# Layer norm closings with a full-array mean, statistics as columns and a diagonal matrix

## The chip, the cores and the metric

One core of one Trainium2 chip runs the whole program. The metric is the device time of one execution in microseconds, smaller is better. The engines are PE (TensorE, products), DVE (VectorE), ACT (ScalarE), POOL (GpSimd) and SP (SyncE, which issues most transfers). Each engine works off its own list of instructions in order.

## What is computed

The program is the backbone of a diffusion transformer: two layers, 256 latent and 256 context tokens of width 1024. Each layer is a half-step feed-forward block, four token mixers side by side, and a second feed-forward block. Every sub-layer ends in a residual with a layer norm behind it, which is what the change is about:

```python
def _norm_f32(x):
    xf = x.astype(jnp.float32)
    mu = jnp.mean(xf, axis=-1, keepdims=True)
    var = jnp.mean(jnp.square(xf - mu), axis=-1, keepdims=True)
    return (xf - mu) * lax.rsqrt(var + LN_EPS)
...
def residual(h, y, mods, s, g, b, r):
    return layer_norm(ALPHA * h + r * mods[..., s, 2, :] * y, g, b)
...
        h_ctx = residual(h_ctx, swiglu_ffn(modulate(h_ctx, mod_c, 0), ffn_w_in[l, 0], ffn_w_out[l, 0]),
                         mod_c, 0, ln_g[l, 0], ln_b[l, 0], FFN_RES)
```

In the last layer the context stream ends inside the mixer, so that mixer 1 and the last feed-forward block work on the 256 latent tokens alone. The convolution mixer has a layer norm of width 512 in its middle.

## The kernel before

**Layout.** Activations are held transposed: `ah` is eight tiles of 128 features (on the partitions) by 512 columns, two *sets* of 256 columns for the two streams. A product in full precision is made as three products of split operands (`xh`, `xl` for the high and low part of the activations, `hi`, `lo` for those of the weights), each a row `mm<-xh,hi` and so on. Products of fp32 operands, as those of the statistics, run as two passes each.

**Order.** The code is written in an order of its own, and a scheduler places the instructions on each engine's list when the program is built; what stands there is what the engine then does, one after another. Inside the mixers a budget (`work`, counted by `mm` and by `counted`) also decides which piece of a branch is written next, so that an operation of another size can move others.

**A norm.** Class `Norm` (L259) serves all layer norms. `arrive(m, cs)` takes in tile m of a residual when it is complete: it squares it (`sq`) and adds the square and the tile itself to running sums `self.q` and `self.s` on DVE (rows `sq<-sq,sq` and `lns<-lns,ah`). `finish(s)` is the *closing* of set s. It sums over the features, which lie on the partitions, by products with a constant matrix `ones[n]` that holds 1/n: four products `st` put mean square and mean as rows onto partitions 0 and 32 of one PSUM tile. ACT copies the mean out (`lnm`, 64x128), DVE squares it and subtracts (`lnv`), ACT takes the root (Sqrt with `eps`), DVE the reciprocal (L311). Row vectors are spread over all partitions by products with a selector, a column of the identity that is broadcast: `bcm` spreads the mean and `bcr` the reciprocal deviation, two products each. `center` subtracts `bcm` from a tile, `scale` multiplies it by `bcr`; ACT then modulates it (`xf`), rounds it (`xh`), and DVE forms the rest (`xl`).

**Where closings stand.** There are 13. Eight belong to four *two-set boundaries* (behind feed-forward block 0 and mixer 0 of layer 0, behind its second block, and behind the first block of layer 1): the set that is complete first is closed first (the *first closing*), and the late output tiles of the other set run as products beside it; then comes the *second closing* in `Boundary.prep` (L431), and the next sub-layer's products have begun on the first set by then. Three stand in the convolution mixers (L772, width 512). Two are *one-set closings*: mixer 1's layer norm (L1159) and the very last, whose scaled tiles are the output. In `ffn` the norm is made at L527.

Of the kernel before, what the change touches and what calls it, by code (L numbers as in the profile page):

```python
# [10 lines left out]
F32 = mybir.dt.float32  # L11
# [6 lines left out]
T = 256  # L18
# [42 lines left out]
def trunk_kernel(ctx: ExitStack, tc: tile.TileContext, I: dict, out: bass.AP):  # L61
# [18 lines left out]
    class Lower:  # L80


        def __init__(self, t):
            self.t = t
# [67 lines left out]
    def sel(r):  # L152

        return ident[0:64, r:r + 1].to_broadcast([64, 128])

# [103 lines left out]
    class Norm:  # L259
# [3 lines left out]
        def __init__(self, n, tiles, pre=False):  # L263
            self.n, self.tiles, self.pre, self.bc = n, tiles, pre, {}

        def arrive(self, m, cs):
# [18 lines left out]
            if m == 0:  # L285
                self.q = sq
            else:
                if m == 1:
                    self.s = blk("lns")
                tt(out=self.q[:, cs], in0=self.q[:, cs], in1=sq[:, cs], op=ALU.add)  # L290
                tt(out=self.s[:, cs], in0=(self.tiles[0] if m == 1 else self.s)[:, cs], in1=d[:, cs], op=ALU.add)

        def finish(self, s):

            H = slice(0, 64)
            p = aux("st")
            for i, x in enumerate((self.q, self.s)):
                for q in range(2):
                    mm(p[32 * q:32 * q + 32, i * 128:i * 128 + 128], ones[self.n][:, 0:32],
                                     x[:, s * T + q * 128:s * T + q * 128 + 128], start=True, stop=True)  # L300
            e2, mu = p[H, 0:128], p[H, 128:256]
            m = sp.tile([64, 128], F32, tag="lnm", name=nm("lnm"), bufs=2)
            v = sp.tile([64, 128], F32, tag="lnv", name=nm("lnv"), bufs=2)
            b, c = aux("bcm"), aux("bcr")
            act(m, mu, AF.Copy)
            tt(out=v, in0=m, in1=m, op=ALU.mult)
            for q in range(2):
                mm(b[:, q * 128:q * 128 + 128], sel(32 * q), m, start=True, stop=True)
            tt(out=v, in0=e2, in1=v, op=ALU.subtract)
            act(v, v, AF.Sqrt, bias=eps[H])  # L310
            V.reciprocal(v, v)  # L311
            for q in range(2):
                mm(c[:, q * 128:q * 128 + 128], sel(32 * q), v, start=True, stop=True)
            self.bc[s] = b[:, 0:T], c[:, 0:T]
# [209 lines left out]
    def ffn(l, w, bd, first, cs, order, np_, nm_=1):  # L524

        s = 2 * w
        nrm = Norm(1024, ah, True)  # L527
# [46 lines left out]
    def mixer(l, bd, cs, sets, order):  # L574
# [584 lines left out]
        nrm = Norm(1024, ah, True)  # L1159
# [161 lines left out]
```

## Time and profile before

| | |
|---|---|
| time, median of 3 runs | 2272.79 us (2269.57 to 2275.2) |
| profiled execution | 2276.33 us, its span 2274.1 us |
| mean granted clock of PE | 0.993 |
| PE busy | 2222.4 us, 98% |
| DVE busy | 1634.6 us, 72% |
| ACT busy | 946.8 us, 42% |
| bytes moved | 323.23 MB, mean 142 GB/s |

The busy times are sums over one profiled execution; the span runs from its first to its last instruction. An engine that is busy 98% of the span sets the time; of the others it matters only where that engine waits for them.

### The profile page before, as it was taken

Reading aid. Unit: us, or ns where it says so; the run is one execution under the profiler, and the core shown is the slowest. Engines: PE = TensorE matmul, PEld = TensorE weight load, DVE = VectorE, ACT = ScalarE, POOL = GpSimd, SP = SyncE. Lnnn points to the kernel's source line nnn. Section 1 sums busy time; section 2 is a strip of 40 time slices with the busy share of each in tenths; the row PEclk is TensorE's granted clock in tenths of the full one; section 3 lists DMA queues with packets and bytes.
Section 4 is the critical chain, followed back from the end, with each engine's and each line's share of the span. In section 5 each row is a group of like instructions: output and inputs, shape, how many; then the busy total and the mean of one; then the engine's idle time right before and its main releaser. Section 6 shows DMA issues by size and latency. Waiting matters only on the chain.

```text
span 2274.1 us, 31541 instructions
## 1 busy us (share of the span) xinstructions
PE 2222.4 (98%) x12216; PEld 1908.5 (84%) x12216; DVE 1634.6 (72%) x2881; ACT 946.8 (42%) x1476; POOL 19.7 (1%) x82
## 2 busy tenths in 40 slices
PE   7999999999999999999999999999999999998997
PEld 4788788888888888888888888888889998998997
DVE  6997865768995754695747488766558989776656
ACT  5322132642345753362222244222326645755443
POOL 2000000000000000000000000000000000000000
PEclk9999999999999999999999999999999999999999
DMA  8665652223222132235535426554534643354653
GB/s 307 214 223 184 204 166 93 98 85 119 85 97 89 57 102 93 84 125 163 168 120 167 139 75 189 181 164 149 160 102 131 190 138 113 121 177 135 197 182 99
DMA packets 94454, 323.23 MB, mean 142 GB/s; under 512 B 10592, under 2 KB 12640, under 8 KB 94304
## 3 DMA queue, kind: packets, MB, share of 16 engines
q1 hardware_dynamic: 94304, 321.22, 43.7%
q8 instruction: 96, 1.57, 0.3%
q14 instruction: 54, 0.44, 0.1%
HBM read 320.12 MB, written 1.05 MB: 141 GB/s over the span
## 4 chain that ended last, share of the span: by engine, by line
PE 89%; DVE 6%; ACT 2%; issue 1%; DMA 1%; SPq 0%; ACTq 0%; DVEq 0%
PE mm L122 84%; DVE lo L113 2%; PE num L122 1%; ACT hi L125 1%; DVE junk L366 1%; DVE junk L216 1%; DVE cacc L113 1%; DVE ah L113 1%; PE gt L122 0%; PE ax L122 0%; PE qk L122 0%; DMA raw<-in_ffn_out 0%; PE bcm L122 0%; DVE sq L113 0%; PE bcr L122 0%
## 5 line engine op out<-in xcount | busy, mean ns | idle before, releaser
L125 ACT ACTIVATE hi<-raw 128x1024 fp32r<-128x1024 f32 (+1 forms) x462 | 474.9, 1031 | 1059.6 <-PE mm L122 709.5
L122 PE MATMUL mm<-xh,hi 128*128 128x512 f32 (+1 forms) x2448 | 847.2, 349 | 7.2 <-ACT hi L125 3.0
L122 PE MATMUL mm<-xh,lo 128*128 128x512 f32 (+1 forms) x2448 | 848.8, 348 | 4.5 <-DVE lo L113 4.5
L122 PE MATMUL mm<-xl,hi 128*128 128x512 f32 (+1 forms) x2448 | 848.4, 347 | 0.0
L113 DVE TENSOR_TENSOR lo<-raw,hi 128x1024 fp32r<-128x1024 f32 (+1 forms) x462 | 546.3, 1186 | 258.3 <-ACT hi L125 255.0
L122 PEld LDWEIGHTS mm<-xh,hi 128*128 128x128 f32 x2448 | 461.9, 190 | 68.3 <-ACT hi L125 5.2
L122 PEld LDWEIGHTS mm<-xh,lo 128*128 128x128 f32 x2448 | 464.4, 190 | 64.4 <-DVE lo L113 6.9
L122 PEld LDWEIGHTS mm<-xl,hi 128*128 128x128 f32 x2448 | 464.9, 190 | 57.0 <-issue 0.7
L122 PE MATMUL mm<-gh,hi 128*128 128x512 f32 (+1 forms) x1600 | 406.6, 344 | 4.2 <-ACT gh L125 2.8
L216 DVE CUSTOM_DVE_ANT_0 junk<-ada,cbc 128x1024 bf16<-128x1024 f32 x256 | 313.0, 1223 | 98.3 <-DMA ada<-in_wada 94.8
L122 PEld LDWEIGHTS mm<-gh,hi 128*128 128x128 f32 x1600 | 277.1, 189 | 46.8 <-ACT gh L125 3.7
L122 PE MATMUL mm<-gh,lo 128*128 128x512 f32 (+1 forms) x800 | 276.0, 345 | 0.0
L122 PEld LDWEIGHTS mm<-gh,lo 128*128 128x128 f32 x800 | 151.1, 189 | 20.2 <-issue 0.7
L113 DVE SCALAR_TENSOR_TENSOR ah<-mm,gate,ah 128x256 f32<-128x256 f32 x192 | 86.1, 480 | 104.5 <-PE mm L122 104.1
L113 DVE SCALAR_TENSOR_TENSOR cacc<-pd,cw,cacc 128x512 f32<-128x512 f32 (+1 forms) x240 | 133.2, 614 | 0.2
L122 PE MATMUL mm<-yh,hi 128*128 128x512 f32 (+1 forms) x512 | 129.3, 339 | 0.0
L113 DVE TENSOR_TENSOR sg<-sg,mm 128x512 f32<-128x512 f32 (+1 forms) x87 | 53.8, 618 | 78.1 <-PE mm L122 77.3
L122 PEld LDWEIGHTS mm<-yh,hi 128*128 128x128 f32 x512 | 88.1, 189 | 11.3
L122 PE MATMUL mm<-yh,lo 128*128 128x512 f32 (+1 forms) x256 | 86.5, 338 | 0.0
L125 ACT ACTIVATE gh<-sg 128x512 fp32r<-128x512 f32 (+1 forms) x88 | 50.5, 574 | 53.2 <-DVE sg L113 52.9
L122 PE MATMUL mm<-mh,hi 128*128 128x256 f32 (+1 forms) x320 | 67.0, 307 | 0.9 <-DVE mh L113 0.6
L125 ACT ACTIVATE xf<-ah,bp,gp 128x256 f32<-128x256 f32 x88 | 48.6, 592 | 24.1 <-DVE ah L113 19.1
(241 smaller groups left out, 1759.8 us busy)
## 6 DMA issues: line engine op xcount, KB each, us to landing
raw<-in_ffn_in SPq DMA_DIRECT2D x176, 512.0 KB, 3.5
ada<-in_wada SPq DMA_DIRECT2D x136, 512.0 KB, 4.0
raw<-in_ffn_out SPq DMA_DIRECT2D x64, 512.0 KB, 3.6
raw<-in_w_G SPq DMA_DIRECT2D x64, 512.0 KB, 3.3
raw<-in_w_br SPq DMA_DIRECT2D x32, 512.0 KB, 3.3
raw<-in_ffn_out SPq DMA_DIRECT2D x32, 384.0 KB, 3.5
raw<-in_w_o SPq DMA_DIRECT2D x24, 512.0 KB, 3.3
shw<-in_wshift SPq DMA_DIRECT2D x16, 256.0 KB, 5.8
```

The lines of the kernel that those rows point to most:

```text
L113: return f(*a, **k)
L122: nc.tensor.matmul(o, w, x, **kw)
L125: S.activation(o, i, f, **kw)
L216: V.tensor_tensor_reduce(out=cur["junk"], in0=w, in1=cur["c"][:, v], scale=1.0, scalar=0.0, op0=ALU.mult, op1=ALU.add, accum_out=m[:, v, t ...
L366: V.tensor_tensor_reduce(out=cur["junk"], in0=w, in1=cur["c"][:, v], scale=1.0, scalar=0.0, op0=ALU.mult, op1=ALU.add, accum_out=m[:, v, k ...
```

## The change

**The mean** is spread by one full-array product of `ones[n]` with the running sum, 256 columns, straight into `bcm`; it reads no result of ACT. **The statistics** are made as columns, tokens on the partitions: products in which the sums are the weights (128 columns) and two columns of `ones[n]` move, four for each pair of sums, into eight columns of `bcr`'s bank beyond the part that is used for the spread. ACT squares the mean (128x4), DVE subtracts, ACT takes the root, DVE the reciprocal, all on 128x4. **The deviation** is spread by way of a diagonal matrix: two DVE operations multiply the identity by the columns of the reciprocal and by n (`dg`, 128x128 each), and one product of `ones[n]` with `dg` gives `bcr`. In norms of one set (`alone`) the last tile and its square aren't added to the sums by DVE: PE adds them up in PSUM, by a second `bcm` product and four more products for the statistics. `sel` goes, a tile `st` less is taken from PSUM in each closing, a block for `dg` more from SBUF.

```diff
...
@@ -260,8 +256,8 @@

 

-        def __init__(self, n, tiles, pre=False):
-            self.n, self.tiles, self.pre, self.bc = n, tiles, pre, {}
+        def __init__(self, n, tiles, pre=False, alone=False):
+            self.n, self.tiles, self.pre, self.alone, self.bc = n, tiles, pre, alone, {}

         def arrive(self, m, cs):
             d = self.tiles[m]
@@ -283,34 +279,41 @@
             if m == len(self.tiles) - 2 and self.pre:
                 act(sp.tile([128, 1], F32, tag="dmy", name=nm("dmy"), bufs=1), sq[:, cs.start:cs.start + 1], AF.Sqrt)
             if m == 0:
-                self.q = sq
+                self.q, self.s = [sq], []
+            elif m == len(self.tiles) - 1 and self.alone:
+
+                self.q.append(sq)
+                self.s.append(d)
             else:
                 if m == 1:
-                    self.s = blk("lns")
-                tt(out=self.q[:, cs], in0=self.q[:, cs], in1=sq[:, cs], op=ALU.add)
-                tt(out=self.s[:, cs], in0=(self.tiles[0] if m == 1 else self.s)[:, cs], in1=d[:, cs], op=ALU.add)
+                    self.s.append(blk("lns"))
+                a, b = self.q[0], self.s[0]
+                tt(out=a[:, cs], in0=a[:, cs], in1=sq[:, cs], op=ALU.add)
+                tt(out=b[:, cs], in0=(self.tiles[0] if m == 1 else b)[:, cs], in1=d[:, cs], op=ALU.add)

         def finish(self, s):

-            H = slice(0, 64)
-            p = aux("st")
-            for i, x in enumerate((self.q, self.s)):
-                for q in range(2):
-                    mm(p[32 * q:32 * q + 32, i * 128:i * 128 + 128], ones[self.n][:, 0:32],
-                                     x[:, s * T + q * 128:s * T + q * 128 + 128], start=True, stop=True)
-            e2, mu = p[H, 0:128], p[H, 128:256]
-            m = sp.tile([64, 128], F32, tag="lnm", name=nm("lnm"), bufs=2)
-            v = sp.tile([64, 128], F32, tag="lnv", name=nm("lnv"), bufs=2)
+            n, cs = self.n, vcols(s)
             b, c = aux("bcm"), aux("bcr")
-            act(m, mu, AF.Copy)
-            tt(out=v, in0=m, in1=m, op=ALU.mult)
-            for q in range(2):
-                mm(b[:, q * 128:q * 128 + 128], sel(32 * q), m, start=True, stop=True)
+            for i, x in enumerate(self.s):
+                mm(b[:, 0:T], ones[n], x[:, cs], start=i == 0, stop=i == len(self.s) - 1)
+
+            ops = [(j, x, t) for i in range(len(self.q)) for j, x in ((0, self.q[i]), (1, self.s[i])) for t in range(2)]
+            for i, (j, x, t) in enumerate(ops):
+                o, k = T + 4 * j + 2 * t, s * T + t * 128
+                mm(c[:, o:o + 2], x[:, k:k + 128], ones[n][:, 0:2], start=i == 0, stop=i == len(ops) - 1)
+            e2, mu = c[:, T:T + 4], c[:, T + 4:T + 8]
+            v = sp.tile([128, 4], F32, tag="lnv", name=nm("lnv"), bufs=2)
+            act(v, mu, AF.Square)
             tt(out=v, in0=e2, in1=v, op=ALU.subtract)
-            act(v, v, AF.Sqrt, bias=eps[H])
+            act(v, v, AF.Sqrt, bias=eps)
             V.reciprocal(v, v)
-            for q in range(2):
-                mm(c[:, q * 128:q * 128 + 128], sel(32 * q), v, start=True, stop=True)
+
+            dg = blk("dg")
+            for t in range(2):
+                ts(out=dg[:, t * 128:t * 128 + 128], in0=ident, scalar1=v[:, 2 * t:2 * t + 1], scalar2=float(n),
+                   op0=ALU.mult, op1=ALU.mult)
+            mm(c[:, 0:T], ones[n], dg[:, 0:T], start=True, stop=True)
             self.bc[s] = b[:, 0:T], c[:, 0:T]

         def center(self, m, s, o):
@@ -524,7 +527,7 @@
     def ffn(l, w, bd, first, cs, order, np_, nm_=1):

         s = 2 * w
-        nrm = Norm(1024, ah, True)
+        nrm = Norm(1024, ah, True, len(order) == 1)
         xh, xl = first[:2] if bd is None else (bd.xh, bd.xl)
         rest = None
         for pi, (j0, j1) in enumerate(PARTS):
@@ -1156,7 +1159,7 @@
             gh.append(a)
             gl.append(b)
         finish_gate(l, 1)
-        nrm = Norm(1024, ah, True)
+        nrm = Norm(1024, ah, True, nset == 1)

         def evac(m, p, c, vs):
             resid(m, p, l, 1, vs)
```

Counted over the program, PE has 26 `bcm`, 26 `bcr` and 52 `st` products fewer, and 15 `bcm` and 13 `bcr` products over 256 columns and 60 two-column products more. DVE has 13 reciprocals and 26 multiplications or subtractions on 64x128 and four additions on 128x256 fewer, and 13 reciprocals, 13 subtractions on 128x4 and 26 `dg` operations more. Three loads of an activation table fewer are on ACT.

PE at the second closing of the first boundary, before (`mm` are products of the next sub-layer on the first set, `st`, `bcm` and `bcr` the closing's; 22 rows of `mm` are left out):

```order
L122 MATMUL mm_2972<-xh_2921,lo_2969 128x256
L122 MATMUL st_3132<-sq_2659,ones_81 32x128 x2
L122 MATMUL st_3132<-lns_2696,ones_81 32x128 x2
L122 MATMUL bcm_3139<-lnm_3137,ident 128x128 x2
L122 MATMUL mm_2951<-xh_2922,hi_2947 128x256
...
L122 MATMUL bcr_3140<-lnv_3138,ident 128x128 x2
L122 MATMUL mm_2972<-xh_2923,lo_2969 128x256
```

and the same place after the change:

```order
L122 MATMUL mm_2972<-xh_2921,lo_2969 128x256
L122 MATMUL bcm_3130<-lns_2696,ones_81 128x256
L122 MATMUL bcr_3131<-ones_81,sq_2659 128x2 x2
L122 MATMUL bcr_3131<-ones_81,lns_2696 128x2 x2
L122 MATMUL bcr_3131<-dg_3142,ones_81 128x256
L122 MATMUL mm_2951<-xh_2922,hi_2947 128x256
L122 MATMUL mm_2958<-xh_2922,hi_2954 128x256
L122 MATMUL mm_2965<-xh_2922,hi_2961 128x256
L122 MATMUL mm_2972<-xh_2922,hi_2968 128x256
L122 MATMUL mm_2951<-xl_2930,hi_2947 128x256
```

Before, 23 rows of `mm` lay between `bcm` and `bcr`; now `bcr` stands directly behind the statistics, and the first row that needs an `xl` is the fifth behind it. The other three boundaries read the same.

DVE at the same closing, before (`ah<-ah,bcr` scales the first set, `ah<-ah,bcm` centers the second):

```order
L113 TENSOR_TENSOR ah_108<-ah_108,bcr_2981 128x256
L113 TENSOR_TENSOR lnv_3138<-lnm_3137 64x128
L113 TENSOR_TENSOR xl_2930<-xf_3150,xh_2922 128x256
L113 TENSOR_TENSOR lnv_3138<-st_3132,lnv_3138 64x128
L113 TENSOR_TENSOR ah_109<-ah_109,bcr_2981 128x256
```

and after the change:

```order
L113 TENSOR_TENSOR lnv_3137<-bcr_3131,lnv_3137 128x4
L113 TENSOR_TENSOR ah_108<-ah_108,bcr_2974 128x256
L310 RECIPROCAL lnv_3137<-lnv_3137 128x4
L113 TENSOR_TENSOR ah_109<-ah_109,bcr_2974 128x256
L113 TENSOR_SCALAR dg_3142<-ident,lnv_3137 128x128 x2
L113 TENSOR_TENSOR ah_102<-ah_102,bcm_3130 128x256
L113 TENSOR_TENSOR ah_103<-ah_103,bcm_3130 128x256
L113 TENSOR_TENSOR ah_104<-ah_104,bcm_3130 128x256
L113 TENSOR_TENSOR xl_2930<-xf_3146,xh_2922 128x256
```

The difference `xl_2930` has moved from the middle of the chain to a place behind `dg` and three centers.

PE in the last mLSTM head of mixer 1, before (`C` is the state's product, `qk` the scores', `M` and `w` spread gates, `num` the numerator; `mm` the dense products of the output branches):

```order
L122 MATMUL mm_16460<-xh_13390,lo_16406 128x256
L122 MATMUL C_16274<-vaug_14908,kw_16263 128x129
L122 MATMUL qk_16281<-q_16153,k_16098 128x256
L122 MATMUL C_16274<-vaug_14908,kw_16263 128x129 x3
L122 MATMUL qk_16281<-q_16153,k_16098 128x256
L122 MATMUL M_16287<-Mw_15571,identr 128x256
L122 MATMUL w_16297<-Mw_15572,identr 128x256
L122 MATMUL M_16300<-Mw_15571,identr 128x256
L122 MATMUL w_16310<-Mw_15572,identr 128x256
L122 MATMUL num_16346<-vaug_14908,E_16291 128x129
```

and after the change, where rows of `mm` lie in the places left out:

```order
L122 MATMUL C_16193<-vaug_14884,kw_16172 128x129 x4
L122 MATMUL qk_16206<-q_16126,k_16079 128x256 x2
...
L122 MATMUL M_16212<-Mw_15547,identr 128x256
L122 MATMUL bcr_16178<-dg_16189,ones_79 128x256
...
L122 MATMUL w_16263<-Mw_15548,identr 128x256
...
L122 MATMUL M_16305<-Mw_15547,identr 128x256
...
L122 MATMUL w_16354<-Mw_15548,identr 128x256
...
L122 MATMUL num_16357<-vaug_14884,E_16216 128x129
```

The rows left out hold 17, 15, 23, 7 and 6 `mm` products; before, none stood between `C` and `num`. The transposes `kT` ahead of them have moved some 70 rows forward.

## Rows read from the trace of the kernel before

**Rows 1.** The page's first part: engine, busy us (share), instructions.

```profile
PE 2222.4 (98%) x12216; PEld 1908.5 (84%) x12216; DVE 1634.6 (72%) x2881; ACT 946.8 (42%) x1476; POOL 19.7 (1%) x82
```

**Rows 2.** PE's waits: line, awaited line, total us, times, longest us.

```profile
PE st L122 <- DVE sq L113: 6.6, 6, 1.8
PE bcr L122 <- DVE lnv L311: 3.4, 2, 1.7
```

**Rows 3.** Like operations elsewhere: tiles `dn`, `bp`; timeline of `hs`, `hT`, `qk`.

```profile
L113 DVE TENSOR_TENSOR dn<-num,dn x24: 127/153/159, 739.0 to 1965.9; 128x2 f32<-128x2 f32 x24
L1051 DVE RECIPROCAL dn<-dn x24: 131/158/168, 739.4 to 1966.5; 128x2 f32<-128x2 f32 x24
...
L125 ACT ACTIVATE bp<-shift,cols x8: 240/262/263, 14.9 to 50.8; 128x2 f32<-128x2 f32 x8
...
805.91 0.86 DVE L113 TENSOR_SCALAR hs<-hs,hmv,hrs 128x128 f32<-128x128 f32 x3
...
861.67 1.25 PE L1090 MATMUL hT<-ident,hs 128*128 128x128 f32 x10
...
1932.39 1.03 PE L122 MATMUL qk<-q,k 128*128 128x256 f32 x4
```

**Rows 4.** Tile `lnv`: shortest, median, longest ns, first and last start.

```profile
L113 DVE TENSOR_TENSOR lnv<-lnm x13: 275/282/285, 398.9 to 2262.7; 64x128 f32<-64x128 f32 x13
...
L311 DVE RECIPROCAL lnv<-lnv x13: 935/939/946, 400.2 to 2264.1; 64x128 f32<-64x128 f32 x13
```

**Rows 5.** Timeline, second closing, first boundary: start, us, instructions, [idle before <-releaser].

```profile
413.73 0.36 PE L122 MATMUL mm<-xh,hi 128*128 128x256 f32 x1 [0.56 <-DVE ah L113]
...
415.23 0.42 DVE L113 TENSOR_TENSOR sq<-sq,sq 128x256 f32<-128x256 f32 x1
...
415.56 1.41 DVE L113 TENSOR_TENSOR ah<-ah,bcr 128x256 f32<-128x256 f32 x4
...
415.79 0.41 PE L122 MATMUL st<-sq,ones 128*32 128x128 f32 x4 [0.76 <-DVE sq L113]
...
416.01 0.41 PE L122 MATMUL st<-lns,ones 128*32 128x128 f32 x4
...
416.82 0.71 PE L122 MATMUL bcm<-lnm,ident 64*128 64x128 f32 x4 [0.40 <-ACT lnm L125]
...
419.00 0.64 PE L122 MATMUL mm<-xh,hi 128*128 128x256 f32 x4
...
420.41 0.71 PE L122 MATMUL bcr<-lnv,ident 64*128 64x128 f32 x4
...
421.05 0.39 PE L122 MATMUL mm<-xh,lo 128*128 128x256 f32 x1
```

**Rows 6.** Timeline, mixer 1's one-set closing.

```profile
2058.88 0.41 PE L122 MATMUL st<-sq,ones 128*32 128x128 f32 x4 [1.80 <-DVE sq L113]
...
2059.55 0.27 ACT L125 ACTIVATE lnm<-st 64x128 f32<-64x128 f32 x1 [1.49 <-PE st L122]
...
2062.45 1.22 PE L122 MATMUL bcr<-lnv,ident 64*128 64x128 f32 x4 [1.70 <-DVE lnv L311]
...
2065.61 1.22 PE L122 MATMUL mm<-xh,hi 128*128 128x256 f32 x4 [1.95 <-ACT xh L125]
```

**Rows 7.** Window behind it: us; PE, PEld, DVE, ACT, POOL busy; PEclk, DMA, GB/s.

```profile
2066.00:2070.00 4.00, 4.00 (x20) 4.00 (x20) 3.54 (x12) 4.00 (x10) 0.00 (x0) 0.50 0.00 0
```

**Rows 8.** Timeline, the last closing.

```profile
2265.11 1.22 PE L122 MATMUL bcr<-lnv,ident 64*128 64x128 f32 x4 [1.70 <-DVE lnv L311]
...
2266.91 1.07 DVE L113 TENSOR_TENSOR ah<-ah,bcr 128x256 f32<-128x256 f32 x3
```

**Rows 9.** Mixer 1's last mLSTM head: timeline of PE, then two windows.

```profile
1960.41 0.38 PE L122 MATMUL w<-Mw,identr 128*128 128x256 f32 x1 [0.78 <-DVE qw L113]
...
1959.00:1963.00 4.00, 2.68 (x11) 2.15 (x11) 3.94 (x10) 4.00 (x12) 0.00 (x0) 0.79 0.38 131
1963.00:1966.00 3.00, 3.00 (x21) 3.00 (x20) 1.60 (x9) 1.78 (x6) 0.00 (x0) 0.72 0.49 164
```

More of the change, by code (lines that the diff above doesn't have):

```diff
@@ L150, in trunk_kernel @@
     masks = const.tile([128, 2, 128], F32, name="masks")
-    def sel(r):
-        return ident[0:64, r:r + 1].to_broadcast([64, 128])
     identr = const.tile([128, 64], F32R, name="identr")
```

## The prediction, made before the changed kernel ran

> **What bounds the kernel now.** I read the page's first part first: PE is busy 98% of the span [rows 1]. A closing can therefore matter in three ways only: by what it costs on PE itself, by the time for which PE stands still for it, and by what a change of order does to other waits. I then read PE's waits by what they wait for [rows 2]. The reader is to see two things there. The product `st` waited six times for the last sum of squares, 6.6 us in all; `bcr` waited for the reciprocal only twice, 3.4 us. With 13 closings this means that `bcr` is reached late enough in eleven of them, and that the two one-set closings (mixer 1's layer norm and the last of the kernel) wait for everything. The stretches themselves come next: a second closing of a two-set boundary, the one-set closing of mixer 1, the last closing and the last mLSTM head of mixer 1, each shown where it is used. The profiled execution took 2276.33 us (span 2274.1), 3.5 us above the median of 2272.79; I make the sum against the first and take 3.5 off.
>
> **Prices of the new operations.** None of them is in the trace in its new place, but each has a near row [rows 3]. DVE subtraction on 128x4: the 128x2 one takes 0.153, so 0.15 us. Reciprocal on 128x4: 0.158 on 128x2, so 0.17. `dg`: `hs` is the same kind and size, three in 0.86, a single one 0.34, so 0.26 apart and about 0.6 for two. ACT Square and Sqrt on 128x4: the 128x2 ACT operation took 0.262. The two-column product loads 128 columns of data as weights and moves next to nothing; the nearest rows are the transposes through `ident`, ten in 1.25, so (1.25 − 0.27)/9 = 0.109 for each of the two passes of an fp32 product, and 8 × 0.109 = 0.87 for the four products of one pair of sums. A product over 256 columns: four passes of `qk` in 1.03, 0.22 apart, 0.44 for one product.
> The Trainium skill, "TensorE: Matmul & The Clock Gate", section "Back-to-back issue gap", gives about 81 ns for a sustained pair of weight load and 128-column product, where the row has 109; by it the four products would take an estimated 0.65 us, and the forecast would be about 1 us lower. I stay with the row, which is fp32 as here.
> What goes: reciprocal 0.939 and two multiplications of 0.28 on DVE [rows 4], and on PE eight `st` passes, 0.63 from first start to last end, and two times four 64-row passes, each 0.64 to 0.71 [rows 5].
>
> **First closings of the four two-set boundaries.** PE has the other set's products to do meanwhile; its cost goes from 0.6 + 0.64 + 0.64, and about 0.4 for the changes between kinds of product, 2.3, to 0.44 + 0.87 + 0.44 and the same changes, 2.2. I set it at nothing; it is hidden by nothing, but it is equal within 0.2. DVE gains: −0.94 − 2 × 0.28 + 0.15 + 0.17 + 0.6 ≈ −0.6 us. At the end of such a boundary DVE is the late engine: PE waits 0.56 for `ah` at 413.73, then 0.76 for the sum of squares [rows 5]. So the second set's sum should be complete about 0.6 us earlier, at 415.05 in place of 415.65.
>
> **Second closings.** Here the order decides. Before, 23 product rows of the other set stand between `bcm` and `bcr`, and they cover the whole chain of deviation. After, `bcr<-dg` stands directly behind the statistics, so PE waits in order for ACT, DVE, ACT, DVE, DVE, and all products behind it wait too. Worked through on the first boundary: PE is free at about 414.5 (0.56 earlier than 415.03), does `bcm` until the sum is there (415.15), statistics until 416.07, 0.1 until ACT has them. Square until 416.43, subtraction 416.6, Sqrt 416.9, reciprocal 417.12; behind it DVE has one scaling by `bcr` in its row (0.34, from the spacing of `ah<-ah,bcr`), so 417.47, then `dg` until 418.07. `bcr` starts at 418.15, products resume at 418.6. They stop once more: after four rows (0.12 each) they need `xl_2930`, which in DVE's new row stands behind three centers: 418.0 + 3 × 0.34 + 0.42 + 0.07 ≈ 419.5. The remaining 19 of the 23 rows then end at 419.5 + 19 × 0.12 = 421.8. Before, the same 23 rows and `bcr` were done at 421.05 [rows 5]. That is **+0.7 each, +2.8 us** for four alike boundaries. Bounds: −0.1 each if the next `xl` is not late and ACT's two steps take 0.15; +1.3 each if the 0.6 us that DVE saves in the first closing does not arrive at the second.
> By the Trainium skill, "VectorE: DVE Perf Modes", section "The TRN2 errata", a small ScalarE operation from PSUM would take 172 cycles and its columns, an estimated 0.15 us where this trace's row has 0.262; the closing would be 0.1 shorter for each. The row is the measurement, so it stands.
>
> **One-set closing of mixer 1.** The change spares the two last DVE additions: `st` waited 1.80 for them until 2058.88 [rows 6]. But in the new order PE does `bcm`, four two-column products, `bcm` again and four more, 2 × (0.44 + 0.87) = 2.6 us. The first half can begin behind the last product, at about 2057.1, the second follows without a gap, so Square starts at about 2059.7; the mean's copy started at 2059.55 before. Nothing is gained up to here. Then Square 0.26, subtraction 0.17, Sqrt 0.28, reciprocal 0.19, `dg` 0.6, `bcr` 0.1 + 0.88 at the half clock: the end is at about 2062.2. Before, `bcr` waited 1.70 for the reciprocal, began at 2062.45 and ended at 2063.67. That is **−1.4 us** for the products that resumed at 2065.61. The granted clock stood at 0.50 in 2066 to 2070 with PE full [rows 7]; those 4 us would be 2 at full speed. A shorter stop may bring the clock back sooner; I take **−0.5** of a range of 0 to −2.
>
> **Last closing.** The same, with eight centers on DVE. Before, the scaling started at 2266.91, held by `bcr` (started 2265.11, took 1.22) and by the centers [rows 8]. After, the chain ends at about 2265, but DVE has 8 × 0.34 + 0.15 + 0.17 + 0.6 = 3.6 us to do from about 2262.4, so it scales from 2266.0: **−0.9** (−0.5 to −1.5).
>
> **The mixers.** The convolution's closings stand among products, and PE hardly waits there; two in mixer 0 and one in mixer 1 are worth 0. But the scheduler moves other work. In mixer 1's last head, before, no dense product stands between the state products `C` and `num`, and from 1959 to 1966 PE was busy 2.68 of 4.00 and 3.00 of 3.00 us at 0.79 and 0.72 of the clock, one wait in it 0.78 for `qw` [rows 9]: 1.32 idle, 2.68 × 0.21 + 3.00 × 0.28 = 1.4 lost to the clock, 2.7 together. After, `kT` comes some 70 rows earlier and `M`, `w` and `num` lie between 23, 15, 23, 7 and 6 product rows. I let all but 0.5 go: **−2.2** (0, if products pulled forward leave a like hole elsewhere, to −2.7).
>
> **Sum.** 2.8 − 1.4 − 0.5 − 0.9 − 2.2 = −2.2 us: 2274.1 for the profiled execution, **2270.6** as a median.
>
> **Rivals.** (1) *The wait in order is dear.* If `bcr<-dg` and the late `xl` cost +2.5 each and mixer 1's head brings nothing, the sum is 10.0 − 2.8 = +7.2, 2280. For it: five hand-overs between engines in a row, where I have only their prices alone. Against: DVE's row shows just one foreign operation in the chain. The kernel gets slower from +1.25 each, if the rest holds: 4 × 1.25 = 5.0. (2) *Everything arrives.* Second closings cost 0.2 each, the clock is up again behind mixer 1's closing, the head's gap is closed: 0.8 − 1.4 − 2.0 − 0.9 − 2.7 = −6.2, and with other small holes that the new order happens to fill 1 to 3 more, 2265. For it: DVE is lighter by 0.6 in each closing, and it is what PE waits for in the boundaries. (3) *The order in the mixers does nothing*, or fills one hole and opens another: 2.8 − 2.8 = 0, 2272.8. For it: the head's products still need ACT and DVE, which were busy 3.94 and 4.00 of the 4 us there.
>
> **How the numbers follow.** Something under 7 us (0.3%) cannot be told from no change here. My case 0.42, rival 3 0.25, rival 2 0.20, rival 1 0.13. The range reaches from 2263, 2 below rival 2, to 2279, which is between rival 3 and rival 1. Faster by over 0.3% (below 2266.0) needs rival 2 with more than its middle: 0.24 with the low tail of mine. Slower by over 0.3% (above 2279.6): rival 1's upper part, 0.10. Between them 0.66.
>
> **What would show it.** In the changed profile PE's waits should list `bcr` behind DVE `dg` four times at 1.5 to 2 us in the boundaries, and `mm` behind DVE `xl` at about 0.4; `st`'s 6.6 us should be gone. In the one-set closings Square should start no earlier than the mean's copy did, and `bcr` end 1.4 earlier. The 128x4 reciprocal should take 0.16 to 0.2. PE should have no hole between `C` and `num` of the last head. I am wrong if `bcr` waits over 2.5 us each, if the two-column products are spaced well off 0.109, or if mixer 0, to which I give nothing, moves by more than 2 us.

## The result

| | median us | runs | ratio to before, 95% interval |
|---|---|---|---|
| before | 2271.86 | 4 | |
| after | 2283.61 (2281.91 to 2285.78) | 4 | 1.0052 [1.0041, 1.0064] |

The change costs 11.75 us, more than the 6.8 us (0.3%) that can be told from no change. The forecast was 2270.6 with a range of 2263 to 2279: the measured time lies outside it, and on the other side of before.

The page of the kernel after has PE busier by 7 us, DVE and ACT a little less busy ([rows 1] before):

```profile
PE 2229.6 (98%) x12184; PEld 1918.4 (84%) x12184; DVE 1625.7 (71%) x2890; ACT 939.4 (41%) x1473; POOL 19.2 (1%) x82
```

**Where the time went.** Both kernels run the same 11352 passes of dense products (`mm`). The start of the nth of them in either trace gives the time by stage, and the same was done for the experiments below. Each column is one profiled execution; the numbers are microseconds more than the profiled execution of before in that stage. B1 to B4 are the two-set boundaries; their rows start some 20 us ahead of the second closing, that of B3 some 90.

```
stage, start in before   after  a_budget b_budget b_half  a_late  a_fill2 a_first b_first hybrid  a_bf   h_bf
ahead of any closing 23  -2.7   -4.5     -2.4     -6.9    -4.6    -6.9    -5.1    -3.3    -6.5    -6.6   -6.9
B1                  389  +1.1   +1.3      0.0      0.0    +2.5    +0.2    -2.1    +2.4     0.0    -2.2   -2.2
products            441  +0.8    0.0     +0.4     +0.2    +0.8    +0.7    +0.6    -0.1     0.0    +0.1   +0.1
mixer 0             646  +6.4   -2.2     +7.7     +0.2    +6.1    +6.3    +6.9     0.0    +0.1    -1.8   +0.5
B2                  957  +1.3   +1.0      0.0     -0.1    +1.9    +0.2    -2.3    +3.7     0.0    -2.3   -2.2
B3                 1269  +0.9   +2.2      0.0     +0.1    +2.7    +0.2    -2.0    +2.2     0.0    -2.1   -2.2
B4                 1707  +1.6   +1.3     -0.1      0.0    +1.8    +0.2    -2.2    +2.3     0.0    -2.4   -2.3
mixer 1            1746  +1.5   +2.5     +4.6     +4.0    +1.8    +1.8    +2.0    +6.3    -0.6    +0.2   +0.2
one-set closing    2037  -1.2   -1.9      0.0     -0.8    -0.9    -0.7    -0.5     0.0    -1.9    -1.6   -1.8
last closing       2254  -1.3   -1.3      0.0      0.0    -1.2    -1.3    -1.3    -0.1    -1.3    -1.3   -1.3
whole span               +8.3   -1.8     +9.8     -3.4   +12.0    +0.5    -6.5   +13.4   -10.4   -18.8  -17.7
```

Stretches of products between the boundaries that differ by at most 1.7 us are left out. The first line is not an effect of any kernel: no closing has run yet. In the profiled execution of before the granted clock fell there at two places (0.79 in 104 to 112 us, 0.86 in 228 to 240 us); in those of the others it fell at one of the two (after and b_first at the second, b_budget at the first) or at neither. Without that line the stages of the kernel after add up to 11.0, which agrees with the medians' 11.75.

So the change gains 2.5 us in the two one-set closings, loses 4.9 in the four boundaries, and loses 6.4 in mixer 0 and 1.5 in mixer 1. The forecast had nothing for mixer 0 and a gain of 2.2 for mixer 1.

**PE's waits after** (columns as in [rows 2]). `st`'s 6.6 us are gone. `bcr` waits in the four boundaries, 1.8 us each, and in the one-set closings as before. The releaser `xf` is inferred by time: the operand that came last is `dg`. New are `w` in mixer 0 and 4.2 us of `cols` in mixer 1 (1.8 before):

```profile
PE bcr L122 <- ACT xf L125: 7.2, 4, 1.8
PE cols L957 <- DVE lf L113: 4.2, 1, 4.2
PE bcr L122 <- DVE dg L113: 3.6, 2, 1.8
...
PE w L122 <- ACT E L125: 2.3, 1, 2.3
```

**The second closing of the first boundary after** (timeline, columns as in [rows 5]; two rows of ACT and one of DVE among those of PE):

```profile
411.48 0.70 PE L122 MATMUL bcm<-lns,ones 128*128 128x256 f32 x2 [0.17 <-DVE lns L113]
412.02 0.50 PE L122 MATMUL bcr<-ones,sq 128*128 128x2 f32 x4
412.38 0.59 PE L122 MATMUL bcr<-ones,lns 128*128 128x2 f32 x4
...
413.01 0.17 ACT L125 ACTIVATE lnv<-bcr 128x4 f32<-128x4 f32 x1 [4.39 <-PE bcr L122]
...
413.61 1.08 ACT L125 ACTIVATE xf<-ah,bp,gp 128x256 f32<-128x256 f32 x2
...
414.14 0.48 DVE L113 TENSOR_SCALAR dg<-ident,lnv 128x128 f32<-128x128 f32 x2
...
414.77 0.69 PE L122 MATMUL bcr<-dg,ones 128*128 128x256 f32 x2 [1.80 <-ACT xf L125]
...
416.38 0.41 PE L122 MATMUL mm<-xh,lo 128*128 128x256 f32 x1
```

and two windows of it (columns as in [rows 7]):

```profile
411.00:415.00 4.00, 2.03 (x14) 1.71 (x13) 3.18 (x13) 1.76 (x6) 0.00 (x0) 1.00 0.36 136
415.00:418.50 3.50, 3.50 (x17) 3.45 (x17) 3.50 (x11) 3.50 (x9) 0.00 (x0) 0.54 0.00 0
```

Three things are to be seen. PE waits 1.80 for the chain, about as forecast. Behind it the clock stands at 0.54 for 3.5 us, near the lower of its two levels (1.2 of 2.4 GHz), and a dense pass then takes 0.41 and not the 0.28 of those ahead of the closing: that was not in the sum. And ACT stood idle for 4.39 us at Square, with the first set's `xf` behind it on its list, although tile `ah_105`, which the first `xf` reads, had been scaled by 410.8 (DVE's row of 410.35, 0.41 long).

**The small operations after** (tile `lnv` and `dg`, shortest, median and longest ns):

```profile
L113 DVE TENSOR_SCALAR dg<-ident,lnv x26: 278/280/286, 397.5 to 2273.4; 128x128 f32<-128x128 f32 x26
L125 ACT ACTIVATE lnv<-bcr x13: 173/174/175, 396.4 to 2272.1; 128x4 f32<-128x4 f32 x13
L113 DVE TENSOR_TENSOR lnv<-bcr,lnv x13: 155/163/164, 396.6 to 2272.3; 128x4 f32<-128x4 f32 x13
L125 ACT ACTIVATE lnv<-lnv,eps x13: 297/297/299, 396.8 to 2272.5; 128x4 f32<-128x4 f32 x13
L310 DVE RECIPROCAL lnv<-lnv x13: 146/178/179, 397.1 to 2272.8; 128x4 f32<-128x4 f32 x13
```

**Mixer 0 after**, the end of its last mLSTM head (timeline of PE and ACT, then two windows):

```profile
792.76 1.28 ACT L125 ACT_TABLE_LOAD   x1
793.68 0.28 PE L122 MATMUL w<-Mw,identr 128*128 128x256 f32 x1
794.28 1.28 ACT L125 ACT_TABLE_LOAD   x1
796.29 0.38 PE L122 MATMUL w<-Mw,identr 128*128 128x256 f32 x1 [2.33 <-ACT E L125]
797.12 0.38 PE L122 MATMUL M<-Mw,identr 128*128 128x256 f32 x1 [0.46 <-ACT E L125]
...
793.00:797.00 4.00, 1.34 (x6) 0.75 (x4) 3.90 (x21) 3.96 (x9) 0.00 (x0) 1.00 0.00 0
797.00:801.00 4.00, 3.88 (x19) 3.88 (x20) 3.05 (x8) 3.95 (x6) 0.00 (x0) 0.57 0.02 4
```

In the kernel before, four microseconds of the same piece of work read

```profile
792.00:796.00 4.00, 4.00 (x25) 3.27 (x24) 3.90 (x21) 3.94 (x8) 0.00 (x0) 1.00 0.01 4
```

PE was full there before. After, it was busy 1.34 of 4 us, with DVE and ACT as busy as ever, and then worked at 0.57 of its clock. It waits 2.33 for ACT's `E`, and ACT's list holds two loads of an activation table ahead of that `E`, 1.28 us each. The kernel before has two such loads in the same piece of work (at 792.62 and 794.13), but there PE has products to do beside them. After, no dense product is left to lie beside the head: behind the last `mm` (793.45) the list holds `w`, `w`, `M`, then 17 rows of `num` with one more `w` among them, 21 rows and 11.9 us to the `hT` that ends the head; before, 11 rows and 4.2 us were left behind the last `mm` (795.67).

**The one-set closing of mixer 1 and the last closing after** ([rows 6] and [rows 8] before):

```profile
2069.90 0.59 PE L122 MATMUL bcr<-ones,ah 128*128 128x2 f32 x4
2070.52 0.17 ACT L125 ACTIVATE lnv<-bcr 128x4 f32<-128x4 f32 x1 [1.60 <-PE bcr L122]
...
2072.28 0.67 PE L122 MATMUL bcr<-dg,ones 128*128 128x256 f32 x2 [1.79 <-DVE dg L113]
...
2074.89 0.58 PE L122 MATMUL mm<-xh,hi 128*128 128x256 f32 x1 [1.95 <-ACT xh L125]
...
2074.00:2078.00 4.00, 3.11 (x14) 3.11 (x15) 3.86 (x13) 4.00 (x11) 0.00 (x0) 0.52 0.00 0
```

From the start of ACT's first step to the first product it is 4.37 us, where before it was 2065.61 − 2059.55 = 6.06; the clock behind it is still 0.52. Part of this difference is the clock's: in 2060 to 2064 of the kernel before it stood at 0.53, and `bcr` took 1.22 [rows 6]; after, it stood at 1.00 in 2070 to 2074, `bcr` took 0.67, and the clock fell only behind the chain.

The last closing ends in DVE's scaling, which after starts 6.0 us behind the last dense product (2269.2) and before 7.3 behind it (2259.6 and 2266.91 [rows 8]):

```profile
2275.24 1.08 DVE L113 TENSOR_TENSOR ah<-ah,bcr 128x256 f32<-128x256 f32 x3
```

### The profile page after: what moved, and what is told of

The parts are those of the page before. It is cut to its first block, busy times and chain, and to the rows that moved or that the text cites. A ratio compares the mean times of both kernels' runs of the same rounds, so it can differ in the third digit from the quotient of the medians.

```text
span 2282.4 us, 31470 instructions
## 1 busy us (share of the span) xinstructions
PE 2229.6 (98%) x12184; PEld 1918.4 (84%) x12184; DVE 1625.7 (71%) x2890; ACT 939.4 (41%) x1473; POOL 19.2 (1%) x82
## 4 chain that ended last, share of the span: by engine, by line
PE 90%; DVE 5%; ACT 3%; DMA 1%; issue 1%; SPq 0%; DVEq 0%; ACTq 0%
PE mm L122 84%; DVE lo L113 2%; PE num L122 1%; ACT hi L125 1%; DMA ada<-in_wada 1%; PE bcr L122 1%; PE ax L122 1%; ACT xf L125 1%; DVE ah L113 1%; PE gt L122 0%; DVE junk L369 0%; PE qk L122 0%; PE bcm L122 0%; DVE junk L212 0%; PE C L122 0%
## 5 line engine op out<-in xcount | busy, mean ns | idle before, releaser
L122 PEld LDWEIGHTS mm<-mh,hi 128*128 128x128 f32 x320 | 51.3, 188 | 5.1 <-DVE mh L113 1.2
```

The source lines that it names most:

```text
L122: nc.tensor.matmul(o, w, x, **kw)
```

## The experiments

The names: a_ is the kernel after, b_ the kernel before, each with one thing changed (a_bf with two). A ratio is taken against runs of before from the same series; kernels of different series are compared by their ratios, since before itself moved by 2 us from one series to another.

### Is it the mixers' budget?

A closing charged the mixers' budget with 1024 columns of fp32 products before and charges it with 520 after (256 for the mean, 8 for the statistics, 256 for the spread); its DVE charge falls as well, from 409 to 355 of the budget's units. Two kernels separate the count from the instructions. a_budget has the changed closings and the old count:

```diff
         def finish(self, s):
+            w0 = dict(work)
...
+            work.update(pe=w0["pe"] + 1024 * 1.69, v=w0["v"] + 2 * (70 + 1.05 * 128))
             self.bc[s] = b[:, 0:T], c[:, 0:T]
```

> The kernel after, with one thing undone: a closing adds to the mixers' budget (the counters that decide which piece of a branch is written next) what it added before the change, 1024 columns of fp32 products and two DVE operations on 64x128, whatever it really issues. The instructions of a closing are all those of the change. Theory (the order in the mixers follows from the counted sizes, and the hole at the end of mixer 0's last mLSTM head is its result): the stretch in mixer 0 that lost 6.4 us and the one in mixer 1 that lost about 1 come back, some 6 to 7.5 us less than after: 2276 to 2278. Rival (the mixers lose by the closings' own instructions, a longer chain or thin products): within 1 us of after, 2283.

Measured: 2272.72 us (2270.8 to 2277.29), 1.001 [1.0001, 1.0019] of before; 10.9 less than after, and below the 2276 expected. In mixer 0 it is 2.2 us faster than before, where after is 6.4 slower. The other half of the theory failed: mixer 1 does not come back but stands at +2.5. b_budget is the mirror image, all instructions of before and the new count (written as 528, 8 more than the kernel after really charges):

```diff
+            work.update(pe=w0["pe"] + 528 * 1.69, v=w0["v"] + 70 + 1.05 * 4 + 2 * (70 + 0.55 * 128))
             self.bc[s] = b[:, 0:T], c[:, 0:T]
```

> The kernel before, all of its instructions kept, but a closing adds to the mixers' budget what it adds after the change (528 columns of fp32 products, one small and two 128-wide DVE operations). Theory (counted sizes): mixer 0 and mixer 1 lose what they lost after, 6 to 7.5 us more than before: 2278 to 2279. Rival (the closings' own instructions): 2272, as before.

Measured: 2283.25 us, 1.0052 [1.0039, 1.0065], the same as the changed kernel to the last digit of the ratio, with not one changed instruction in a closing; above the 2279 expected. The loss is 7.7 us in mixer 0 and 4.6 in mixer 1, and next to nothing anywhere else. PE shows the same hole in mixer 0 (timeline and a window of b_budget):

```profile
796.23 0.38 PE L122 MATMUL w<-Mw,identr 128*128 128x256 f32 x1 [2.32 <-ACT E L125]
...
803.25 0.82 PE L122 MATMUL num<-vaug,E 128*128 128x129 f32 x4 [0.75 <-DVE E L113]
...
795.00:800.00 5.00, 3.32 (x14) 3.12 (x15) 3.68 (x14) 4.94 (x11) 0.00 (x0) 0.71 0.01 3
```

That the count makes mixer 0's loss is settled by the two from both sides. In mixer 1 the new count alone costs 4.6, but the old count does not take the loss away, so the count is not the whole of it there. That b_budget equals after as a whole is a coincidence of other terms, as the stage table shows: after loses less in mixer 1, loses in the boundaries and gains in the one-set closings.

b_half charges a closing about halfway, 776 columns:

> The kernel before with the mixers' budget charged halfway between before and after for each closing (776 columns in place of 1024 and 528). If the loss grows with the charge that is missing, it is about half of the 11.6 us: 2275 to 2278. If it hangs on which piece falls behind the end of the dense work, as a step: within 1.5 us of before or of the full 11.6, 2270 to 2272 or 2282 to 2284.

Measured: 2275.07 us, 1.002 [1.0011, 1.0028]. The total is near the half, and would have passed for a loss in proportion. The stages say otherwise: mixer 0 loses 0.2 of b_budget's 7.7, mixer 1 loses 4.0 of its 4.6. Neither loss grows in proportion, as the theory of a step has it, and the total fell in the range of the other theory by the sum of the two. Where the steps lie no run shows.

### Is it the place of the spread in the boundaries?

a_late puts `bcr<-dg` of the second closings 24 product rows later on PE's list, and changes nothing else in PE's order but three pairs of neighbours:

```diff
     def mmk(tiles, xh, xl, c, nrm=None):
...
+            if k == 5 and nrm is not None and nrm.held:
+                with tc.issue_after(ins.ins):
+                    nrm.held()
```

> The kernel after, with the product that spreads the deviation, in the second closing of the four two-set boundaries alone, put on PE's list 24 product rows later (behind the fifth k of the next sub-layer's products on the first set); nothing else of PE's order is moved in the boundaries. Theory (PE's wait in order for dg, and the low clock behind it, make the boundaries' loss of 1.3 to 2.0 us each): the four waits of 1.8 us and the half clock behind them vanish, 5 to 7 us less than after: 2277 to 2278.5. Rival (the loss is the thin products' and DVE's new row, xl behind three centers): at most 2 us less, 2281.5 to 2283.5.

Measured: 2284.16 us, 1.0059 [1.0046, 1.0071]: no gain over after, in the boundaries 0.2 to 1.8 us more each (+2.5, +1.9, +2.7, +1.8). The theory that the wait in order is the loss fell here. The timeline of a_late (ACT, then PE) and a window say why:

```profile
410.98 0.17 ACT L125 ACTIVATE lnv<-bcr 128x4 f32<-128x4 f32 x1 [4.39 <-PE bcr L122]
411.38 0.30 ACT L125 ACTIVATE lnv<-lnv,eps 128x4 f32<-128x4 f32 x1 [0.23 <-DVE lnv L113]
411.59 1.08 ACT L125 ACTIVATE xf<-ah,bp,gp 128x256 f32<-128x256 f32 x2
...
413.02 1.23 PE L122 MATMUL mm<-xh,hi 128*128 128x256 f32 x4 [2.08 <-ACT xh L125]
...
411.00:415.00 4.00, 1.98 (x9) 1.96 (x10) 3.77 (x14) 3.77 (x11) 0.00 (x0) 0.63 0.00 0
```

The product that no longer waits for `dg` is gone from its place, and the next one has nothing to work on: its `xh` comes from ACT, and ACT held `xf` back behind Square for 4.39 us. One wait had covered another of 2.08. The clock falls all the same.

### ACT's order

New theory: the closing's Square and Sqrt stand on ACT ahead of the first set's modulations, and hold them. a_first writes the first set's remaining tiles ahead of the second closing:

```diff
                 for w, go in self.rest:
                     go()
-                    self.nrm.finish(w)
                 self.apply(v, range(HEAD, 8))
+                for w, _ in self.rest:
+                    self.nrm.finish(w)
```

> The kernel after, with two steps of a two-set boundary written in the other order: the first set's remaining five tiles are scaled, modulated and split ahead of the second closing, not behind it. On ACT the five xf and their xh then stand ahead of Square and Sqrt, on DVE two of the five xl ahead of the subtraction, and on PE the spread stands 43 product rows later. New theory, after moving the spread alone gave nothing (PE then waited 2.1 us for xh, since ACT had sat 4.4 us at Square, in order, with the first set's modulations behind it): the boundaries lose by ACT's order. Expected: PE's waits of 1.8 us (bcr) and 2.1 us (xh) both go, the clock in the boundaries stays at full, 5 to 6 us less than after, 2278 to 2279. Rival (the loss lies in the thin products and DVE's row): 2282 to 2284.

Measured: 2266.49 us (2264.53 to 2269.35), 0.9987 [0.9978, 0.9996]; by the ratios about 15 us less than after, over twice what was expected, and 13.5 of it in the four boundaries. Each boundary is now 2.0 to 2.3 us shorter than in the kernel before: the loss of 0.9 to 1.6 has gone, and so have the waits that before had at `mm` for `ah`, at `st` and at `bcm`, 0.56 + 0.76 + 0.40 [rows 5]. ACT and a window of a_first:

```profile
408.10 0.60 ACT L125 ACTIVATE xf<-ah,bp,gp 128x256 f32<-128x256 f32 x1 [2.18 <-DVE ah L113]
...
410.31 0.17 ACT L125 ACTIVATE lnv<-bcr 128x4 f32<-128x4 f32 x1 [0.18 <-PE bcr L122]
...
408.00:412.00 4.00, 3.83 (x31) 3.57 (x30) 3.89 (x13) 3.69 (x10) 0.00 (x0) 1.00 0.42 154
```

`xf` starts ahead of Square, ACT waits 0.18 in place of 4.39, PE's only wait is 0.17 at `bcm`, and the clock stays at 1.00. Mixer 0 keeps its loss (6.9). The swap moved rows on ACT, DVE and PE together (the spread stands 43 product rows later as well); that ACT's part decides is an inference from a_late, where PE's part alone gave nothing. No kernel moved ACT's order alone.

Is the swap good for itself? b_first is the kernel before with the same lines:

> The kernel before with the same swap in the two-set boundaries: the first set's remaining tiles written ahead of the second closing; no closing is changed. In the kernel after the swap was worth 17 us, some 3.7 at each boundary, more than the 1.5 that each had lost. If the gain of the swap belongs to the order alone, before gains as much or the most of it (each boundary held waits of 0.8, 0.6 and 0.4 on PE): 2260 to 2264. If the swap pays only with the short chain of the changed closing (ACT and DVE free soon enough): at most 1 us each, 2267 to 2271.

Measured: 2286.18 us, 1.0062 [1.0049, 1.0076]: slower by 15.6 (about 14 by the ratio), an answer that neither expectation held. The boundaries lose 2.2 to 3.7 each, mixer 1 6.3. PE of b_first (timeline and a window):

```profile
412.36 0.41 PE L122 MATMUL st<-sq,ones 128*32 128x128 f32 x4 [0.76 <-DVE sq L113]
414.03 0.74 PE L122 MATMUL mm<-xh,hi 128*128 128x256 f32 x4 [1.04 <-ACT xh L125]
...
416.00:420.00 4.00, 4.00 (x24) 3.65 (x23) 2.17 (x7) 3.64 (x9) 0.00 (x0) 0.71 0.01 2
```

`st` still waits 0.76 for the sum of squares, then PE waits for `xh`, and the clock falls to 0.71. The clock is not the whole of it: at B3 it stayed at 1.00, PE waited 2.2 for `xh` in two pieces, and the boundary lost the same 2.2. So the order of the boundary and the kind of closing belong together: the same swap is worth −3.4 each with the changed closing and +2.7 with the old one. Why the scheduler's list with the old closing leaves PE without `xh` was not followed further.

### The clock

a_fill puts 14 dense products that nobody reads into PE's wait, between the statistics and the spread:

```diff
+                f = aux("fill")
+                for i in range(14):
+                    with tc.issue_after(ins.ins):
+                        ins = nc.tensor.matmul(f[:, 0:T], fill[:, T:T + 128], fill[:, T:T + T], start=True, stop=True)
```

> The kernel after, with 14 products of 256 columns that nobody reads (first tile of the first set with itself) on PE between the statistics and the spread of each of the four second closings, about 1.7 us of dense work in the 1.8 us in which PE waits there. ACT and DVE have the same chain to do. If the granted clock falls behind the closing (0.54 in 415 to 418.5 in the kernel after) because PE did nothing dense from 411 to 415, it stays at 1.0 and the rows behind run 0.12 apart, not 0.21: some 0.7 to 1.3 us less for each boundary, 3 to 5 in all, 2278.5 to 2281. If the clock is not what makes the boundaries slow (ACT's order starves PE anyway), 2283 to 2285.

Measured: 2283.07 us, as the rival has it, but it doesn't decide: the filling products waited 1.4 us each time for a PSUM buffer, so that the pause was there as before, only ahead of them. Its trace still holds a comparison. With the same rows in all four boundaries, the clock fell behind the pause at B1 and B3, which lost 2.3 and 2.4 us against before, and stayed at 1.00 at B2 and B4, which lost 0.8 each. That prices the low clock at about 1.6 a boundary. Two windows of a_fill, behind the closings of B2 and B3:

```profile
988.00:992.00 4.00, 4.00 (x35) 3.95 (x34) 4.00 (x13) 4.00 (x11) 0.00 (x0) 1.00 0.01 2
1362.00:1366.00 4.00, 4.00 (x22) 3.82 (x22) 4.00 (x14) 4.00 (x10) 0.00 (x0) 0.60 0.02 6
```

a_fill2 writes into the unused half of the mean's tile (`b[:, T:T + T]`) and differs from after by the 14 products alone:

> Again the kernel after with 14 dense products that nobody reads between the statistics and the spread of the four second closings, now into the unused half of the mean's PSUM tile, so that they wait for no buffer (in the first try they stood 1.4 us for one); no other row of PE and none of ACT is moved. If the clock falls behind the closing because PE has nothing dense to do there, it now stays at 1.0 and the rows behind run at 0.12, not 0.21: 0.7 to 1.3 us less each, 2278.5 to 2281. If the supply of xh and xl sets the time there, not the clock: 2282 to 2284.

Measured: 2277.01 us (2275.81 to 2278.2), 1.0027 [1.0016, 1.0037]; 6.6 less than after by the medians, 5.7 by the ratios, 4.1 of it in the four boundaries. PE of a_fill2 (timeline, then two windows; this execution ran about 4 us earlier):

```profile
408.79 1.92 PE L308 MATMUL bcm<-xh 128*128 128x256 f32 x14
410.72 0.67 PE L122 MATMUL bcr<-dg,ones 128*128 128x256 f32 x2
...
412.21 0.39 PE L122 MATMUL mm<-xl,hi 128*128 128x256 f32 x1 [0.34 <-DVE xl L113]
...
408.00:411.00 3.00, 2.98 (x24) 2.79 (x23) 2.01 (x9) 1.81 (x6) 0.00 (x0) 1.00 0.12 44
411.00:415.00 4.00, 3.66 (x29) 3.41 (x28) 4.00 (x13) 4.00 (x10) 0.00 (x0) 1.00 0.00 0
```

With useless work in the wait the clock stays at 1.00, and a boundary costs 0.2 more than before, not 0.9 to 1.6. The wait for `dg` by itself thus costs next to nothing against the waits that it took the place of: in the first boundary PE waits 1.80 + 0.17 after, 0.56 + 0.76 + 0.40 before. 0.7 to 1.4 us at each boundary are the half clock. And the late `xl` of the prediction shows here, 0.34 at the fifth row behind `bcr`; in the kernel after, at half clock, the four rows ahead of it took 1.03 us (415.08 to 416.11), and PE did not stop there.

### The one-set closings alone, and both repairs

hybrid has the changed closing in the two one-set norms only, and before's in the eleven others:

> The kernel before, with the changed closing (and its sums on PE) in the two one-set norms alone, mixer 1's layer norm and the last of the kernel; all other closings, and so the mixers' order, are those of before. Theory (the one-set closings gain 1.2 and 1.4 us, as the profile after shows, and nothing else does): 2.6 us less than before, 2269.2. Rival (that gain came with the moved order ahead of them, or is lost to the clock): 2272, as before.

Measured: 2267.72 us, 0.9982 [0.9973, 0.9991], 4 us less than before: −1.9 and −1.3 in the two closings and −0.6 in mixer 1. This −0.6 comes with the very instructions of before, so it shows how far two executions differ. No moved order ahead of mixer 1's closing can have made the gain there, since PE, ACT and DVE have before's rows up to it. How much of the 1.9 belongs to the closing is less clear, because the clock differs: hybrid's `bcr` took 1.19 at the half clock as before's did, but the clock was back sooner (0.70 in 2058 to 2062); b_half, with before's own closing, stands at −0.8 in that stage, since its `bcr` ran at full clock (0.71); and a_first, a_late and a_fill2 gain only 0.5 to 0.9. By these some 0.5 to 1.2 us are the closing's, an estimate, and the rest is the clock's. a_bf takes both repairs, the old count and the swap:

> The kernel after with both repairs: a closing counts in the mixers' budget as it did before the change, and the first set's remaining tiles are written ahead of the second closing. Theory (the two losses are separate and add): 2272.7 less 5 to 6, 2266.5 to 2268; with the gains of the one-set closings and of lighter boundaries it is below the kernel before by 4 to 5. Rival (the boundaries give nothing): 2272 to 2273.

Measured: 2256.19 us (2254.94 to 2257.09), 0.9942 [0.9929, 0.9954]: 13.6 us less than before, about 25 less than after by the ratios, and 10 below what was expected: each boundary gains 3.3 to 4.3 against a_budget, and mixer 1's loss is gone. This is the fastest kernel of the study. h_bf keeps before's closing in the convolution's norms:

> The changed closing in all norms of width 1024 (boundaries with the first set's tiles written ahead, and the one-set norms), the closing of before in the convolution's three norms, and the mixers' budget counted as before, so that the mixers' order is that of before as far as the scheduler lets it. If the changed closing in the boundaries is worth something of its own once ACT is free of it (four sums of squares that PE awaited 0.8 us each, DVE lighter by 0.6): 2264 to 2266, below the 2267.7 of the kernel with only the one-set closings changed. If not: 2267 to 2269.

Measured: 2258.37 us, 0.9952 [0.994, 0.9965], below the 2264 to 2266 of its theory: each boundary gains 2.2 to 2.3 against before and hybrid. The difference of 2 us from a_bf lies in mixer 0 (−1.8 and +0.5).

## Why the prediction was wrong

**Mixer 0: the step that failed.** The prediction said of the convolution's closings that they "stand among products, and PE hardly waits there; two in mixer 0 and one in mixer 1 are worth 0", and under what would make it wrong "if mixer 0, to which I give nothing, moves by more than 2 us". It moved by 6.4. The closings themselves are indeed worth nothing or a gain there (a_budget: −2.2). What was missed is that a closing is also counted: with about 500 columns less charged for each, the pieces are written in another order, and the last head falls behind the dense products. b_budget loses 7.7 there with every instruction of before's closings. The order of the two kernels showed it, had mixer 0's last head been read as mixer 1's was: no `mm` between `w`, `M` and `num`. Reading that one place only, because PE waited there before, looked for holes where they were and not where new ones might come. Rival 3 ("fills one hole and opens another") had the mechanism and priced it at 0 for want of that look. Measured against the forecast's −2.2, the stages of after are 13 us off: 6.4 by mixer 0, 3.7 by mixer 1 (−2.2 forecast, +1.5 measured), 2.1 by the boundaries, the rest by smaller terms.

**Mixer 1.** The gap that the prediction meant to close did close: in the kernel after PE was busy all of 1959 to 1971 at the full clock, and up to 1976 it waits once, 0.62 for `qw`. The mixer still lost 1.5, where the forecast was −2.2, and what grew there is another wait. `cols`, the transposes of the gates, waits for DVE's `lf`; after (timeline of PE, and the window in which the wait ends):

```profile
1902.67 0.37 PE L957 MATMUL cols<-ident,lf 64*128 64x64 f32 x1 [4.17 <-DVE lf L113]
1900.00:1904.00 4.00, 1.32 (x7) 1.11 (x8) 3.87 (x9) 2.58 (x5) 0.13 (x2) 0.51 0.42 131
```

and before:

```profile
1889.97 0.27 PE L954 MATMUL cols<-ident,lf 64*128 64x64 f32 x1 [1.81 <-DVE lf L113]
1888.00:1892.00 4.00, 2.19 (x13) 1.71 (x13) 3.92 (x8) 2.39 (x5) 0.13 (x2) 1.00 0.41 135
```

Behind the wait of 4.17 the clock is 0.51, then 0.64 in 1904 to 1908; behind that of 1.81 it stays at 1.00, in 1892 to 1896 too. Over the kernels the two go together: where `cols` waits 4.1 to 4.2, mixer 1 is at +1.5 to +6.3 (after, a_budget, b_budget, b_half, a_late, a_fill, a_fill2, a_first, b_first), where it waits 1.8 to 1.9, at −0.6 to +0.2 (hybrid, a_bf, h_bf). What brings `lf` late in each order no run shows: a_budget has the long wait with the old count, b_first with before's closings. The rest of the spread, up to 6.3, stays open too.

**Second closings.** Forecast +0.7 each, measured +0.9 to +1.6, but not by the forecast's sum. The wait was rightly foreseen (1.80, the sum had 2.08 from the statistics' end to `bcr`). The late `xl` that was to cost another stop cost 0.34 in a_fill2, where the clock was full, and nothing at the half clock of the kernel after. The missing term is the clock, 0.7 to 1.4 each by a_fill2. The prediction had the order rows of PE and DVE, and those of ACT would have shown `lnv` ahead of `xf`. As far as a_late and a_first show, ACT's idle 4.39 us lies behind both the wait and the low clock; ACT's order was not moved by itself.

**Prices.** The two-column passes came 0.36 apart for four, 0.09 each, for a forecast of 0.109. The Trainium skill, "TensorE: Matmul & The Clock Gate", section "Back-to-back issue gap", has 81 ns for a sustained pair of weight load and 128-column product: the trace lies between the page and the row that was preferred. Square took 0.174 where the row gave 0.262. The estimate from the Trainium skill, "VectorE: DVE Perf Modes", section "The TRN2 errata", was 0.15, and was the nearer here. Sqrt took 0.297 (forecast 0.26), the subtraction 0.163, the reciprocal 0.178, the two `dg` 0.48 (forecast 0.6). None of these decided anything.

**One-set closings.** Forecast −1.4 − 0.5 and −0.9, measured −1.2 and −1.3 (hybrid: −1.9 and −1.3). Square started no earlier, as forecast, and the chain behind it is shorter; but part of what the table shows is the clock's place, as said with hybrid. The clock was not back sooner in the kernel after: it stood at 0.52 in 2074 to 2078 and 0.63 in 2078 to 2082 behind the chain, where before's was at 0.94 in 2070 to 2074.

**Rivals.** Rival 1, the dear wait at +2.5 a boundary, came near the measured total with its 2280, but by luck: no boundary cost more than 1.6, and it had nothing for mixer 0. The range was too narrow because the orders in the mixers were taken to be worth between −2.7 and 0, when the order had been read at one place out of two.

## What to carry to other kernels

Where sizes of operations feed a budget that sets the order, a change of sizes moves work far from the edit: give the new operation the old count first (a_budget), and read what is left. Take off a wait only after asking what the product behind it waits for, and read the lists of all engines of a chain: here the third one, ACT, held the operands. A short wait can cost twice, once itself and once in the clock behind it; useless products in the pause tell the two apart, if they wait for no buffer themselves.

## What was not expected of the hardware

In the kernel after, the clock fell behind a wait of 1.80 us that came after 0.95 us of thin products (two columns moved by each pass), to 0.54 over the next 3.5 us. In the kernel before, waits of 0.56, 0.76 and 0.40 in the same place left it at 1.00 (4.5 of 4.5 us busy behind them). With 14 products of 256 columns in the pause it stayed at 1.00.

The length of a wait alone does not tell whether the clock falls. In a_fill the same rows were followed by a fall at two boundaries and by none at the other two. The wait of 1.8 us at mixer 1's `cols` left the clock at 1.00 in the kernel before, and in hybrid, with the same rows, was followed by 0.87 and 0.71 (1880 to 1884 and 1884 to 1888).
